# Moving the modulation columns of a two-layer decoder trunk between stages, and its first accumulating DMAs behind the sums of squares

## The chip, the core and the metric

The kernel runs on one core of a Trainium2 chip. The metric is device time in microseconds (us) of one execution. Five engines matter: PE (TensorE, the matmuls; PEld is its weight load), DVE (VectorE), ACT (ScalarE), POOL (GpSimd) and SP (SyncE, which here only issues DMAs). Each has its own list of instructions, fixed when the kernel is built, and goes through it in that order; a wait at the head of a list holds up what stands behind it.

## The reference

A decoder trunk of two layers on 1024 tokens of width 1024, in f32. Each layer is

```
mod = silu(c) @ ada_w[i] + ada_b[i];   sh1, sc1, g1, sh2, sc2, g2 = split(mod, 6)
h   = rmsnorm(x, norm1_g) * (1 + sc1) + sh1
x   = x + g1 * (mixers(h @ w_in) @ w_out)        # SSD scan, pooling, dilated attention
h   = rmsnorm(x, norm2_g) * (1 + sc2) + sh2
x   = x + g2 * (silu(g) * u @ ffn_down),  g, u = conv3(h @ ffn_up)
```

and a last rmsnorm. `mod` is a vector of 6144 numbers for each layer: 48 columns of 128 in the kernel, 8 columns for each of the six parts (part 0 is sh1, 1 sc1, 2 g1, 3 sh2, 4 sc2, 5 g2).

## The kernel before, in words

Activations lie transposed, 128 channels by 1024 tokens in a tile. A matmul in f32 is made of three with weights and activations split in a high and a low half: `hi*hi`, `hi*lo`, `lo*hi` (lines 232 to 234, or 966 to 968 in the up projection). Each weight block of 128x512 is loaded by SP, its high half is cast by ACT (L161) and its low half is subtracted by DVE (L162), so that ACT and DVE are busy beside PE all the time.

A layer has four stages. The **mixer** follows a table by hand, `ORDER`: projections of the input (tiles `qk`, `B`, `C`, `xs`, `z`, `u`), attention, scan, norm and pooling, interleaved. The **output projection** ends it: a first half (tile `dq`) in `accum_group`, a second half (`dn`) in `accum_last`. The latter goes over the eight blocks of x twice, once for each half of the tokens; each block's square is summed up for the rmsnorm (`square_add`, L187; on POOL for blocks 1 to 6, on DVE for block 7), and when the sum is done `rstd_begin` lets PE add it over partitions (tile `ssps`, L203). The **up projection** (`ffn`) runs 22 units f, in a form with seven half-size products each (tiles `px`, `pv`); a unit's convolutions, silu and product are four DVE instructions on `fg` and `fu` (L1120) and one product `fg*fu` (L1161) at its end, whose result goes to DRAM. The **down projection** reads it back, in five groups of `accum_group` (`dq`) and an `accum_last` (`dn`).

Four weights of a unit are sums of blocks of `ffn_up`, and are added by DMAs that accumulate, issued from POOL (`plus`, L1011): S1 and S3 each get a block added, S2 gets S1, S4 gets S2. `prepare(0)` and `prepare(1)` issue those of the first two units, eight in all, ahead of `accum_last` of the output projection.

A column of `mod` (`ada_col`, L137) takes two loads of 128x512 by SP (tile `araw`) and two DVE instructions (L143) that multiply and sum them up. `araw` takes one of the two buffers of `raw`, which it shares with the weight blocks; in the down projection it takes one of the 16 buffers of a ring (`wr`). Part 0 and 1 of layer 0 are made at the start by other means. The other 80 columns stand in these places:

- mixer of layer 0: 24 columns, parts 2, 4 and 3 of layer 0 (the `A` entries of `ORDER`)
- up projection of layer 0: 12 columns, one in each unit from 7 to 18: part 5 of layer 0, then the first four of layer 1
- down projection of layer 0: the other 44 of layer 1, in `accum_group` of the groups 1 to 4
- layer 1: none

The program is written in the order of the code, but the build's scheduler then sets each engine's list by priorities and modelled times, so that instructions stand earlier in the list than the code says where it finds the engine idle.

Of the kernel before, what the change touches and what calls it, by code (L numbers as in the profile page):

```python
# [8 lines left out]
F32 = mybir.dt.float32  # L9
# [45 lines left out]
def tile_trunk(ctx, tc, xT_d, c_d, ck_d, adas_d, pos_d, par_d, pff_d, fg_d, adaw_d, win_d, wv_d, poolw_d, wout_d, up_d, down2_d, down_d,  # L55
# [82 lines left out]
    def ada_col(l, j, take=None):  # L138

        for i in range(2):  # L140
            r = take("araw") if take else rawp.tile([128, 528], F32, tag="raw", name="araw")[:, 0:512]
            nc.sync.dma_start(r, adaw_d[l, j, :, HALF[i]])
            dve.scalar_tensor_tensor(r, r, 1.0, cact[:, HALF[i]], ALU.mult, ALU.mult,  # L143
                                     accum_out=mod[l][:, j:j + 1] if i == 0 else mod2[:, j % 8:j % 8 + 1])
        if j % 8 == 7:
            s = slice(j - 7, j + 1)
            dve.tensor_tensor(mod[l][:, s], mod[l][:, s], mod2, op=ALU.add)
            ada_fin(l, j // 8, 0, 8)
# [270 lines left out]
    def layer(l, hi, lo, end, st):  # L419
# [390 lines left out]
        todo = [p * 8 + k for p in (2, 4, 3) for k in range(8)] if l == 0 else []  # L810
# [29 lines left out]
        for t in ORDER.split():  # L840
            if t[0] in "BCXzu":
                project(t)
            elif t[0] == "A":
                for _ in range(int(t[1:])):
                    if todo:
                        ada_col(0, todo.pop(0))
# [22 lines left out]
    def ffn(l, ys, end):  # L869
# [134 lines left out]

        def prepare(f):
# [4 lines left out]
            def plus(t, src):  # L1010
                nc.gpsimd.dma_start(t, src, accum_op=ALU.add)  # L1011
# [119 lines left out]
        accum_last(wout_d[l, 1], ys, 16, l, None, PARTS[0], first_half, begin, second_half, store)  # L1131

        todo = [(0, 40 + k) for k in range(8)] + [(1, p * 8 + k) for p in (1, 0, 2, 4, 3, 5) for k in range(8)] if l == 0 else []

        def ada(n, take=None):
            for _ in range(n):
                if todo:
                    ada_col(*todo.pop(0), take)
# [25 lines left out]
        for f in range(NFF + 1):  # L1164
# [5 lines left out]
            if 6 < f < 19:  # L1170
                ada(1)
# [8 lines left out]
        for g, n in enumerate(GROUPS):  # L1180
# [4 lines left out]
            else:  # L1185
                m = acts(fs, ht) if g else m0
                for i, _ in enumerate(accum_group(down_d[l, g] if n == 4 else down2_d[l], m, 40, l, () if g else pre)):
                    if g:
                        ada(1 + (n > 2 and i % 2), wr)
# [26 lines left out]
    def accum_last(src, m, gcol, l, dep, parts, then, early, rest=None, store=None):  # L1216
# [4 lines left out]
        for hs in parts:  # L1221
            acc = p2("acc", "nr", 2)[:, 0:hs.stop - hs.start]
            for n in range(8):
# [9 lines left out]
                square_add(acc, x[n][:, hs], n == 0, nc.gpsimd if rest and n < 7 else dve)  # L1233
                if done and not early:
                    then(n, *done)
# [142 lines left out]
```

## Time and profile before

| | us |
|---|---|
| median of 3 runs | 2293.74 (2292.01 to 2296.97) |
| profiled execution | 2290.45 |
| its span, first to last instruction | 2288.6 |
| PE busy | 2227.4 (97%) |
| DVE busy | 1549.4 (68%) |
| ACT busy | 1058.9 (46%) |
| POOL busy | 242.4 (11%) |
| mean granted PE clock | 0.990 |

How to read it: "x24" is a count, "128x512" a tile's partitions and elements, "<-" leads from what is written to what is read. In a timeline row the first number is the start, the second the duration, and a bracket at its end gives the idle time of the engine just before it and what ended it. The two layers run the same stages one after the other, so that a stage of layer 0 can be set beside the same stage of layer 1.

### The profile page before, as it was taken

The numbers are of one execution on the slowest core, as the hardware profiler recorded it, in microseconds if no ns is written. First come the engines' busy times: TensorE is split into PE (matmuls) and PEld (weight loads), VectorE is DVE, ScalarE is ACT, GpSimd is POOL, SyncE is SP. The second block draws the span as 40 slices with busy tenths as digits, with TensorE's granted clock in tenths as the row PEclk, the third lists the DMA queues.
The fourth block names the chain that finished last, engine by engine and source line by source line (L and its number), as shares of the span: only waits on it lengthen the run. The fifth ranks groups of instructions, "written<-read, shape, count | busy, mean of one in ns | idle before, by whom it ended". The sixth has DMA issues, their size and how long they took to land.

```text
span 2288.6 us, 29727 instructions
## 1 busy us (share of the span) xinstructions
PE 2227.4 (97%) x10472; PEld 1809.1 (79%) x10472; DVE 1549.4 (68%) x2712; ACT 1058.9 (46%) x1960; POOL 242.4 (11%) x308
## 2 busy tenths in 40 slices
PE   6999999899999999999999999998999999999998
PEld 4878877687788888788888888776888888878887
DVE  6467887588766667995564577774976666675446
ACT  5366664355444545312244667533654554452212
POOL 0210000231111110000001000003211111100000
PEclk9999999999999999999999999998999999999999
DMA  7452333558787776992233211235777767673112
GB/s 274 126 150 77 95 111 127 161 147 223 209 201 176 176 174 193 340 310 63 58 132 109 57 55 48 83 107 173 178 186 179 179 171 180 162 246 103 50 46 88
DMA packets 186228, 338.93 MB, mean 148 GB/s; under 512 B 28704, under 2 KB 44320, under 8 KB 186080
## 3 DMA queue, kind: packets, MB, share of 16 engines
q1 hardware_dynamic: 126144, 244.44, 32.8%
q0 software_dynamic: 30560, 61.56, 14.9%
q10 hardware_dynamic: 29376, 31.05, 4.1%
q8 instruction: 82, 1.34, 0.2%
q14 instruction: 66, 0.54, 0.1%
HBM read 265.93 MB, written 44.83 MB: 136 GB/s over the span
## 4 chain that ended last, share of the span: by engine, by line
PE 67%; DVE 2%; DMA 2%; ACT 0%; issue 0%; POOL 0%; SPq 0%; ACTq 0%; DVEq 0%; POOLq 0%
PE dq L232 6%; PE dq L233 6%; PE dq L234 6%; PE px L966 6%; PE px L967 6%; PE px L968 6%; PE pv L966 4%; PE pv L967 4%; PE pv L968 4%; PE dn L234 1%; PE dn L232 1%; PE dn L233 1%; PE qk L232 1%; PE qk L233 1%; PE qk L234 1%; PE z L232 1%
## 5 line engine op out<-in xcount | busy, mean ns | idle before, releaser
L161 ACT CAST whi<-wraw 128x512 fp32r<-128x512 f32 (+2 forms) x196 | 117.6, 602 | 398.4 <-PE dq L233 268.3
L232 PE MATMUL dq<-ah,whi 128*128 128x512 f32 x576 | 226.9, 394 | 1.9 <-DVE xd L1213 1.2
L233 PE MATMUL dq<-al,whi 128*128 128x512 f32 x576 | 226.6, 393 | 0.0
L234 PE MATMUL dq<-ah,wlo 128*128 128x512 f32 x576 | 225.8, 393 | 0.0
L161 ACT CAST whi<-S 128x512 fp32r<-128x512 f32 x176 | 108.7, 620 | 213.8 <-PE px L967 124.5
L162 DVE TENSOR_TENSOR wlo<-wraw,whi 128x512 fp32r<-128x512 f32 (+2 forms) x196 | 132.0, 677 | 106.8 <-ACT whi L161 102.1
L1213 DVE SCALAR_TENSOR_TENSOR xd<-dq,mod,xd 128x1024 f32<-128x1024 f32 x80 | 102.7, 1284 | 127.1 <-PE dq L234 127.1
L162 DVE TENSOR_TENSOR wlo<-S,whi 128x512 fp32r<-128x512 f32 x176 | 120.8, 688 | 80.3 <-ACT whi L161 78.1
L966 PE MATMUL px<-T24h,whi 128*128 128x512 f32 x352 | 139.7, 397 | 4.7 <-ACT s L1029 3.2
L143 DVE SCALAR_TENSOR_TENSOR araw<-araw,cact 128x512 f32<-128x512 f32 x160 | 106.5, 690 | 52.9 <-DMA araw<-in_adaw 52.9
L968 PE MATMUL px<-T24h,wlo 128*128 128x512 f32 x352 | 138.9, 395 | 1.3 <-DVE wlo L162 1.3
L967 PE MATMUL px<-T24l,whi 128*128 128x512 f32 x352 | 139.0, 395 | 0.0
L966 PE MATMUL pv<-B,whi 128*128 128x512 f32 x344 | 135.7, 395 | 0.0
L967 PE MATMUL pv<-B,whi 128*128 128x512 f32 x344 | 135.5, 394 | 0.0
L968 PE MATMUL pv<-B,wlo 128*128 128x512 f32 x344 | 135.0, 393 | 0.0
L1120 DVE SCALAR_TENSOR_TENSOR fg<-G,pff,fg 128x1023 f32<-128x1023 f32 x88 | 112.7, 1281 | 26.5 <-ACT fg L1118 26.4
L232 PEld LDWEIGHTS dq<-ah,whi 128*128 128x128 f32 x576 | 108.3, 188 | 28.0 <-ACT whi L161 1.8
L161 ACT CAST whi<-A 128x512 fp32r<-128x512 f32 x118 | 73.2, 620 | 120.5 <-PE pv L967 58.0
L234 PEld LDWEIGHTS dq<-ah,wlo 128*128 128x128 f32 x576 | 108.3, 188 | 25.1 <-DVE wlo L162 0.5
L233 PEld LDWEIGHTS dq<-al,whi 128*128 128x128 f32 x576 | 108.4, 188 | 24.0
L162 DVE TENSOR_TENSOR wlo<-A,whi 128x512 fp32r<-128x512 f32 x118 | 81.0, 686 | 63.2 <-ACT whi L161 54.6
L1011 POOL DMA_DIRECT2D S<-S x88 | 75.4, 869 | 426.0 <-DMA S<-in_up 309.6
(403 smaller groups left out, 5883.1 us busy)
## 6 DMA issues: line engine op xcount, KB each, us to landing
S<-in_up SPq DMA_DIRECT2D x176, 256.0 KB, 3.1
araw<-in_adaw SPq DMA_DIRECT2D x160, 256.0 KB, 4.2
A<-in_up SPq DMA_DIRECT2D x118, 256.0 KB, 3.7
S<-in_up POOLq DMA_DIRECT2D x88, 256.0 KB, 5.5
S<-S POOLq DMA_DIRECT2D x88, 256.0 KB, 4.1
raw<-act_d SPq DMA_DIRECT2D x88, 256.0 KB, 4.1
act_d<-fg SPq DMA_DIRECT2D x40, 512.0 KB, 3.8
wraw<-in_down SPq DMA_DIRECT2D x80, 256.0 KB, 2.8
```

What stands on the lines that cost most here:

```text
L143: dve.scalar_tensor_tensor(r, r, 1.0, cact[:, HALF[i]], ALU.mult, ALU.mult, accum_out=mod[l][:, j:j + 1] if i == 0 else mod2[:, j % 8:j % ...
L161: act.copy(hi[:, 0:n], raw)
L162: dve.tensor_tensor(lo[:, 0:n], raw, hi[:, 0:n].bitcast(F32), op=ALU.subtract)
L232: mm(ps, wh, hi[k][:, s], start=i == 0, stop=False)
L233: mm(ps, wh, lo[k][:, s], start=False, stop=False)
L234: mm(ps, wl, hi[k][:, s], start=False, stop=i == n - 1)
L966: after(mm(ps, wh[:, c], h_, start=first and k == 0, stop=False, skip_group_check=not first), dep)
L967: mm(ps, wh[:, c], l_, start=False, stop=False, skip_group_check=not first)
L968: mm(ps, wl[:, c], h_, start=False, stop=k == 3, skip_group_check=not first)
L1011: nc.gpsimd.dma_start(t, src, accum_op=ALU.add)
L1120: dve.scalar_tensor_tensor(acc[:, s:T], t[:, 0:T - s], pff[:, (2 - s) * 44 + cc:(2 - s) * 44 + cc + 1], acc[:, s:T], ALU.mult, ALU.add)
L1213: group_last[0] = dve.scalar_tensor_tensor(x[n], ps, mod[l][:, gcol + n:gcol + n + 1], x[n], ALU.mult, ALU.add)
```

## The change

Two edits. The accumulating DMAs of units 0 and 1 are put on a list, `pending`, and taken off it one by one in `accum_last`, in its second half of the tokens, each behind a block's sum of squares. And the 80 columns are spread anew: mixer of layer 0 24 as before, up projection of layer 0 24 (units 3 to 20, two in every third), down projection none, mixer of layer 1 24, up projection of layer 1 8. All of them take the two `raw` buffers.

```
-        todo = [p * 8 + k for p in (2, 4, 3) for k in range(8)] if l == 0 else []
+        todo = [p * 8 + k for p in (2, 4, 3) for k in range(8)]
...
-                        ada_col(0, todo.pop(0))
+                        ada_col(l, todo.pop(0))
...
+        pending = []
+
+        def sums(part, n):
+
+            if part and pending and n < 7:
+                pending.pop(0)()
+                if n == 6:
+                    while pending:
+                        pending.pop(0)()
...
-                nc.gpsimd.dma_start(t, src, accum_op=ALU.add)
+                add = lambda: nc.gpsimd.dma_start(t, src, accum_op=ALU.add)
+                if f < 2:
+                    pending.append(add)
+                else:
+                    add()
...
-        todo = [(0, 40 + k) for k in range(8)] + [(1, p * 8 + k) for p in (1, 0, 2, 4, 3, 5) for k in range(8)] if l == 0 else []
+        todo = [(l, 40 + k) for k in range(8)] + ([(1, p * 8 + k) for p in (1, 0) for k in range(8)] if l == 0 else [])
...
-            if 6 < f < 19:
-                ada(1)
+            if 2 < f < 21:
+                ada(1 + (f % 3 == 0))
...
-                for i, _ in enumerate(accum_group(down_d[l, g] if n == 4 else down2_d[l], m, 40, l, () if g else pre)):
-                    if g:
-                        ada(1 + (n > 2 and i % 2), wr)
+                for _ in accum_group(down_d[l, g] if n == 4 else down2_d[l], m, 40, l, () if g else pre):
+                    pass
...
                 square_add(acc, x[n][:, hs], n == 0, nc.gpsimd if rest and n < 7 else dve)
+                if sums:
+                    sums(hs.start, n)
```

What the build makes of it in the engines' lists is seen at three places. First, POOL in the output projection of layer 1, before; `S..<-in_up` and `S..<-S..` are the accumulating DMAs of units 0 and 1, `acc` the sums of squares of the first half of the tokens:

```order
L1011 DMA S_13411<-in_up 128x512
L1011 DMA S_13415<-in_up 128x512
L1011 DMA S_13413<-S_13411 128x512
L187 TENSOR_TENSOR acc<-acc,sq 128x512
L1011 DMA S_13425<-in_up 128x512
L1011 DMA S_13422<-S_13413 128x512
L1011 DMA S_13429<-in_up 128x512
L1011 DMA S_13427<-S_13425 128x512
L187 TENSOR_TENSOR acc<-acc,sq 128x512 x2
L1011 DMA S_13436<-S_13427 128x512
L187 TENSOR_TENSOR acc<-acc,sq 128x512 x9
```

And the same place in the changed kernel:

```order
L1021 DMA S_13361<-in_up 128x512
L1021 DMA S_13365<-in_up 128x512
L1021 DMA S_13363<-S_13361 128x512
L187 TENSOR_TENSOR acc<-acc,sq 128x512
L1021 DMA S_13371<-in_up 128x512
L1021 DMA S_13369<-S_13363 128x512
L187 TENSOR_TENSOR acc<-acc,sq 128x512
L1021 DMA S_13375<-in_up 128x512
L1021 DMA S_13373<-S_13371 128x512
L187 TENSOR_TENSOR acc<-acc,sq 128x512
L1021 DMA S_13379<-S_13373 128x512
L187 TENSOR_TENSOR acc<-acc,sq 128x512 x9
```

Nine sums behind the last DMA are three of the first half of the tokens and the six of the second half. All eight DMAs stand ahead of those three, before and after; one sum stands two DMAs earlier. In layer 0 seven of the eight stand ahead of the first half's last two sums before, and of its last one after; the eighth stands behind all six in both.

Second, DVE in the up projection of layer 0, in the unit whose `fg*fu` is the eighth, before; `wlo` is the low half of a weight block:

```order
L162 TENSOR_TENSOR wlo_5693<-S3_5598,whi_5692 128x512
L162 TENSOR_TENSOR wlo_5712<-A12_5605,whi_5711 128x512
L162 TENSOR_TENSOR wlo_5729<-S1_5594,whi_5728 128x512
L1034 TENSOR_TENSOR G_5582<-pv_5565,U2_5500 128x512
L162 TENSOR_TENSOR wlo_5774<-A11_5754,whi_5773 128x512
```

And in the changed kernel:

```order
L162 TENSOR_TENSOR wlo_5729<-S3_5634,whi_5728 128x512
L143 SCALAR_TENSOR_TENSOR araw_6447,mod2_103<-araw_6447,cact_97 128x512
L143 SCALAR_TENSOR_TENSOR araw_6606,mod1_102<-araw_6606,cact_97 128x512
L162 TENSOR_TENSOR wlo_5748<-A12_5641,whi_5747 128x512
L143 SCALAR_TENSOR_TENSOR araw_6609,mod2_103<-araw_6609,cact_97 128x512
L162 TENSOR_TENSOR wlo_5765<-S1_5630,whi_5764 128x512
L143 SCALAR_TENSOR_TENSOR araw_6767,mod1_102<-araw_6767,cact_97 128x512
L1048 TENSOR_TENSOR G_5618<-pv_5601,U2_5536 128x512
L162 TENSOR_TENSOR wlo_5812<-A11_5792,whi_5811 128x512
L143 SCALAR_TENSOR_TENSOR araw_6770,mod2_103<-araw_6770,cact_97 128x512
```

Five column instructions now stand in this unit. Counted between one `fg*fu` and the next, the column instructions in layer 0 were 2, 2, 6, 5, 6, 3 and are now 2, 2, 6, 6, 5, 6, 5, 6, 5, 5; in layer 1 they were none and are now 2, 2, 6, 6.

Third, DVE in the mixer of layer 1, where `dts` is what ACT and PE wait for to begin the scan; before:

```order
L162 TENSOR_TENSOR wlo_10764<-wraw_10761,whi_10763 128x512
L518 COPY acs_10571<-acsps_10568 128x64
L162 TENSOR_TENSOR wlo_10770<-wraw_10767,whi_10769 128x512
L522 TENSOR_TENSOR dts_10575<-acsps_10568,acs_10571 128x64
L551 TENSOR_TENSOR kk0_10597<-qk1_10286,kk0_10597 64x1024
```

And in the changed kernel:

```order
L162 TENSOR_TENSOR wlo_10575<-wraw_10572,whi_10574 128x512
L518 COPY acs_10370<-acsps_10367 128x64
L162 TENSOR_TENSOR wlo_10581<-wraw_10578,whi_10580 128x512
L143 SCALAR_TENSOR_TENSOR araw_10735,mod1_102<-araw_10735,cact_97 128x512
L143 SCALAR_TENSOR_TENSOR araw_10738,mod2_103<-araw_10738,cact_97 128x512
L143 SCALAR_TENSOR_TENSOR araw_10791,mod1_102<-araw_10791,cact_97 128x512
L522 TENSOR_TENSOR dts_10374<-acsps_10367,acs_10370 128x64
L551 TENSOR_TENSOR kk0_10396<-qk1_10085,kk0_10396 64x1024
```

Three column instructions now stand ahead of `dts`, as they do in layer 0 (before and after). From the copy of `acs` to the start of the second half of the output projection, DVE's and PE's lists in the two layers of the changed kernel are the same, row for row, but for one small set-up instruction (L423, a 128x40 scaling for the next layer).

More of the change, by code (lines that the diff above doesn't have):

```diff
@@ L136, in tile_trunk, with ada_col @@
     act.activation(cact, cact, AF.Silu)
-    def ada_col(l, j, take=None):
+    def ada_col(l, j):
         for i in range(2):
-            r = take("araw") if take else rawp.tile([128, 528], F32, tag="raw", name="araw")[:, 0:512]
+            r = rawp.tile([128, 528], F32, tag="raw", name="araw")[:, 0:512]
             nc.sync.dma_start(r, adaw_d[l, j, :, HALF[i]])
@@ L1130, in ffn, with ada @@
         prepare(1)
-        accum_last(wout_d[l, 1], ys, 16, l, None, PARTS[0], first_half, begin, second_half, store)
-        todo = [(0, 40 + k) for k in range(8)] + [(1, p * 8 + k) for p in (1, 0, 2, 4, 3, 5) for k in range(8)] if l == 0 else []
-        def ada(n, take=None):
+        accum_last(wout_d[l, 1], ys, 16, l, None, PARTS[0], first_half, begin, second_half, store, sums)
+        todo = [(l, 40 + k) for k in range(8)] + ([(1, p * 8 + k) for p in (1, 0) for k in range(8)] if l == 0 else [])
+        def ada(n):
             for _ in range(n):
                 if todo:
-                    ada_col(*todo.pop(0), take)
+                    ada_col(*todo.pop(0))
         def acts(fs, pool):
@@ L1214, in accum_group, with accum_last @@
             yield
-    def accum_last(src, m, gcol, l, dep, parts, then, early, rest=None, store=None):
+    def accum_last(src, m, gcol, l, dep, parts, then, early, rest=None, store=None, sums=None):
         mh, ml = zip(*m)
```

## Prediction

> **What bounds the kernel now.** I read the page first: shares of the engines, the chain that ended last, the costliest groups.
>
> ```profile
> span 2288.6 us, 29727 instructions
> PE 2227.4 (97%) x10472; PEld 1809.1 (79%) x10472; DVE 1549.4 (68%) x2712; ACT 1058.9 (46%) x1960; POOL 242.4 (11%) x308
> PE 67%; DVE 2%; DMA 2%; ACT 0%; issue 0%; POOL 0%; SPq 0%; ACTq 0%; DVEq 0%; POOLq 0%
> L143 DVE SCALAR_TENSOR_TENSOR araw<-araw,cact 128x512 f32<-128x512 f32 x160 | 106.5, 690 | 52.9 <-DMA araw<-in_adaw 52.9
> ```
>
> PE sets the time, and is idle for 2288.6 - 2227.4 = 61.2 us. The change touches no matmul, so it can only open or close gaps on PE. A column is two of the L143 instructions, 0.69 us each, and the last figure is what counts: DVE stood still 52.9 us in front of them, waiting for their loads, with everything behind them in its list waiting too.
>
> The two layers run the same stages, layer 0 with columns, layer 1 with none. So I looked up where each stage begins, by the first matmul of its tile: scan part of the mixer (B), output projection (dn), up projection (px), down projection (dq), its last part (dn).
>
> ```profile
> L232 PE MATMUL B<-h1h,whi x32: 392/396/774, 112.1 to 223.6; 128*128 128x512 f32 x32
> L232 PE MATMUL dn<-yh,whi x32: 389/394/628, 424.0 to 468.5; 128*128 128x512 f32 x32
> L966 PE MATMUL px<-B,whi x80: 389/394/404, 480.3 to 895.7; 128*128 128x512 f32 x80
> L232 PE MATMUL dq<-ah,whi x288: 389/392/501, 918.6 to 1118.8; 128*128 128x512 f32 x144
> L232 PE MATMUL dn<-ah,whi x32: 389/394/481, 1119.5 to 1154.1; 128*128 128x512 f32 x32
> L232 PE MATMUL B<-h1h,whi x32: 387/396/482, 1236.9 to 1342.1; 128*128 128x512 f32 x32
> L232 PE MATMUL dn<-yh,whi x32: 389/393/628, 1538.9 to 1587.5; 128*128 128x512 f32 x32
> L966 PE MATMUL px<-B,whi x80: 389/394/404, 1599.3 to 2006.1; 128*128 128x512 f32 x80
> L232 PE MATMUL dq<-ah,whi x288: 389/392/469, 2029.0 to 2229.0; 128*128 128x512 f32 x144
> L232 PE MATMUL dn<-ah,whi x48: 276/283/404, 2229.7 to 2271.6; 128*128 128x256 f32 x32, 128*128 128x512 f32 x16
> ```
>
> Then the busy time of the engines in these stretches, layer 0 above layer 1 in each pair.
>
> ```profile
> core 0: us, PE busy (x) PEld busy (x) DVE busy (x) ACT busy (x) POOL busy (x), PEclk, DMA share, GB/s
> 112.10:424.00 311.90, 304.45 (x1602) 247.07 (x1602) 244.86 (x589) 183.56 (x442) 14.41 (x27) 0.98 0.36 108
> 1236.90:1538.90 302.00, 300.94 (x1603) 243.40 (x1603) 217.60 (x492) 186.66 (x444) 14.43 (x27) 1.00 0.25 73
> 424.00:480.30 56.30, 49.78 (x209) 40.02 (x208) 30.21 (x46) 19.36 (x33) 21.27 (x19) 0.94 0.64 180
> 1538.90:1599.30 60.40, 51.60 (x210) 41.56 (x209) 30.23 (x46) 19.30 (x33) 21.17 (x19) 0.89 0.57 168
> 480.30:918.60 438.30, 432.32 (x1866) 349.48 (x1865) 313.80 (x437) 226.41 (x341) 75.09 (x86) 1.00 0.75 193
> 1599.30:2029.00 429.70, 429.44 (x1865) 348.74 (x1864) 298.52 (x379) 228.01 (x342) 75.65 (x86) 1.00 0.71 183
> 918.60:1119.50 200.90, 199.97 (x865) 162.12 (x864) 152.84 (x305) 45.28 (x78) 1.05 (x2) 1.00 0.61 205
> 2029.00:2229.70 200.70, 199.69 (x866) 162.38 (x865) 100.20 (x121) 45.29 (x77) 0.55 (x1) 1.00 0.29 90
> ```
>
> This is an experiment already made. Same matmuls in each pair, and the columns' price is the difference: mixer 311.9 - 302.0 = 9.9 us for 24 columns; up projection 438.3 - 429.7 = 8.6 us for 12; down projection 200.9 - 200.7 = 0.2 us for nearly all of 44. In the down projection DVE was full of columns (152.8 against 100.2 us) and PE did not notice, since it needs DVE there only once in a block. The change takes the columns from the one stage where they are free.
>
> **The change part by part: columns in the up projection.** DVE's product fg*fu ends a unit, so its starts show how fast DVE goes from unit to unit. The first row is a stall of PE, the next are from DVE's timeline, the last from the instruction's statistics over a stretch without columns.
>
> ```profile
> 539.47 0.50 PE L966 MATMUL px<-T24h,whi 128*128 128x512 f32 x1 [1.50 <-ACT U L1029]
> 557.91 1.22 DVE L1161 TENSOR_TENSOR fg<-fg,fu 128x1024 f32<-128x1024 f32 x1
> 581.14 1.22 DVE L1161 TENSOR_TENSOR fg<-fg,fu 128x1024 f32<-128x1024 f32 x1
> 603.49 1.23 DVE L1161 TENSOR_TENSOR fg<-fg,fu 128x1024 f32<-128x1024 f32 x1
> 611.95 0.69 DVE L143 SCALAR_TENSOR_TENSOR araw<-araw,cact 128x512 f32<-128x512 f32 x1 [4.66 <-DMA araw<-in_adaw]
> 625.68 1.22 DVE L1161 TENSOR_TENSOR fg<-fg,fu 128x1024 f32<-128x1024 f32 x1
> 645.89 1.22 DVE L1161 TENSOR_TENSOR fg<-fg,fu 128x1024 f32<-128x1024 f32 x1
> 662.18 1.22 DVE L1161 TENSOR_TENSOR fg<-fg,fu 128x1024 f32<-128x1024 f32 x1
> L1161 DVE TENSOR_TENSOR fg<-fg,fu x13: 1220/1222/1233, 662.2 to 895.3; 128x1024 f32<-128x1024 f32 x13
> ```
>
> A clean unit takes (895.3 - 662.2) / 12 = 19.43 us, PE's pace. Units with 6, 5 and 6 column instructions took 23.23, 22.35 and 22.19 us, one with 3 took 20.21: DVE falls behind by 3.8, 2.9, 2.8 and 0.8, together 10.3, and catches up 3.1 in the next clean one (16.29). The reason is in the row at 611.95: two buffers hold two loads, the third column instruction of a unit waits for a load that could only be issued once the first was used. Late sums on DVE hold up ACT's copies and the weights' low halves, and PE stalls. Check: 10.3 - 3.1 and the stall of 1.5 at 539.47, which layer 1 lacks, make 8.7, against 8.6 measured.
>
> In the changed kernel the list has the same pattern, but for eight such units in layer 0 (6, 6, 5, 6, 5, 6, 5, 5) instead of 6, 5, 6, 3. Slack is spent by then, so each further unit costs what the last full one did, 22.19 - 19.43 = 2.8: four units 11.1, and the one with 3 becomes a full one, 2.0. Sum **+13.1 us**. Bounds: by the column, 12 x 8.6 / 12 = 8.6; by the slowest unit, 5 x 3.8 = 19.0.
>
> Layer 1 gets 2, 2, 6, 6: 3.8 + 2.9 - 3.1 caught up + 1.5 = **+5.1 us**. Bounds: 1.5, if the two full units fit into the slack, and 3.8 x 2 - 3.1 + 1.5 = 6.0.
>
> **Columns in the mixer.** Mixer 1 gets the 24 columns in mixer 0's very order, so I take mixer 0's time: **+9.9 us**. The first stall below says what that consists of (the other two rows are for the accumulating DMAs).
>
> ```profile
> 120.85 0.61 PE L529 MATMUL acsTp<-ident,acs 128*8 128x128 f32 x4 [3.23 <-DVE dts L522]
> 456.64 1.87 PE L203 MATMUL ssps<-ones,acc 128*128 128x1 f32 x8 [3.88 <-DVE acc L187]
> 1575.28 1.02 PE L203 MATMUL ssps<-ones,acc 128*128 128x1 f32 x4 [6.67 <-DVE acc L187]
> ```
>
> PE's idle time in mixer 0 is 311.90 - 304.45 = 7.45 us against 302.00 - 300.94 = 1.06 in mixer 1; the stall of 3.23 is `dts` queued behind three column instructions. The other 3.5 us lie in PE's busy time, with a granted clock of 0.98 against 1.00. The Trainium skill (TensorE: Matmul & The Clock Gate, What's actually happening) has the clock fall only after an idle window of about 3.4 us; by that these 3.5 us would not come again and the term would be 6.4. Here the clock fell although the longest stall of the stage lasted 3.23 us. Bounds: 6.4, the idle time alone; above, 12, if the weight loads that share the two buffers come later still.
>
> **Down projection.** 44 columns out: 0.2 us back, at most 200.90 - 199.97 = 0.9, PE's whole idle time there. DVE's 52.6 us that go away lay beside PE's matmuls; nobody there waits for them.
>
> **Accumulating DMAs.** What they cost is seen on POOL in the output projection of layer 1 (start, duration, idle before):
>
> ```profile
> 1561.54 0.99 POOL L1011 DMA_DIRECT2D S<-S  x1
> 1562.11 3.13 POOL L187 TENSOR_TENSOR acc<-acc,sq 128x512 f32<-128x512 f32 x2
> 1569.65 0.87 POOL L1011 DMA_DIRECT2D S<-S  x1 [4.42 <-DMA S<-S]
> 1570.26 4.24 POOL L187 TENSOR_TENSOR acc<-acc,sq 128x512 f32<-128x512 f32 x3
> ```
>
> The last issue must wait until the one of 1561.54 has landed, 8.1 us later; three sums stand behind it, then DVE's, then PE's 6.67 us of stall. The code now issues these DMAs behind the second half's sums, but the build's list still has all of them, that issue included, ahead of the same three sums. The DMA it waits for moves behind one more sum, so its landing slips by up to 1.4 us (4.24 / 3), about +0.9 in layer 1. In layer 0 one sum less stands behind the seventh DMA, about -0.9. Taken as **0**, from -2.8 to +2.8 (one sum in each layer, either way). POOL's own list has nothing else there, and units 0 and 1 use these weights only after 480.3.
>
> **Sum.** 13.1 + 5.1 + 9.9 - 0.2 + 0 = +27.9 us. The profiled execution took 2290.45 us (span 2288.6 and 1.85 around it), so 2318.35 on its scale; the median of the runs, 2293.74, lies 3.29 above it, and with that the forecast is **2321.6 us**, 1.2% slower.
>
> **The rivals.** First, the sums come free: if the eight DMAs do go late, PE's 3.88 and 6.67 go, 10.6, and with them part of what the clocks of 0.94 and 0.89 take off 56.3 and 60.4 us (3.4 and 6.6): about -14, that is 2307.6. For it, the stalls are real; against it, POOL's list, in which nothing decisive moved. Still slower. 5%.
>
> Second, only busy time counts: DVE was busy 313.8 of 438.3 us in the up projection and 244.9 of 311.9 in mixer 0, so columns fit everywhere and the +8.6 and +9.9 are layer 0's own (its first units, its tables). Then the result is 2293.5, no change. The Trainium skill (Perfetto Trace Analysis, Identifying the Most-Contended Engine) says that for VectorE the occupancy is a fair measure of how close it is to its limit; by that page this rival would hold. The trace speaks against it: a DVE busy at 72% was late by 2.8 us and more in each full unit, because it waits in order. 5%.
>
> Third, on the other side, loads that arrive in time: DVE's waits for `araw` vanish in the up projections because SP's list differs a little. The point is the third load of a unit: it would have to land before 607.3 (611.95 - 4.66), where DVE ran dry, not at 611.95. Then layer 0's 8.6 us go as well, layer 1 pays nothing, and mixer 1 pays its idle time without the stall behind the loads, 6.4 - 3.2 = 3.2: 2293.74 - 8.6 + 3.2 - 0.2 = 2288.1, faster by 0.25%. Against it: still two buffers, still six instructions in a unit. 5%.
>
> **How the numbers follow.** The forecast, columns paid as in layer 0, has 85%. Its low ends add to 8.6 + 1.5 + 6.4 - 0.9 - 2.8 = 12.8, its high ends to 19.0 + 6.0 + 12 + 2.8 = 39.8. The range is 2306 to 2334, which takes in the first rival. A measurement of this kernel can tell about 0.2%, 4.6 us, from no change: slower 0.90 (forecast and first rival), same 0.05 (second), faster 0.05 (third).
>
> **What would show it.** Right: DVE's fg*fu at 22 us distance over eight units of layer 0, with 4 to 5 us waits for `araw` in each; the up projection of layer 0 near 451 us and of layer 1 near 435, mixer 1 near 312 with PE stalled some 3 us at `acsTp`; down projections alike at 200.7; stalls at `ssps` still 3 to 4 and 6 to 7 us. Wrong: distances back at 19.4 us after the first units (columns then cost by start-up, not by number), mixer 1 still near 302, or `ssps` without its wait.

## The result and the profile after

The changed kernel takes 2317.73 us (median; 2315.3 to 2320.89) against 2294.67 us of the kernel before, run beside it: a ratio of 1.0104, 95% interval 1.0092 to 1.0115, that is 23 us slower. The forecast was 2321.6 us, and slower. The profiled execution of the changed kernel took 2315.77 us, 25.3 more than that of the kernel before.

The page of the changed kernel, three of its lines: the span, the busy times, and the group of the column instructions.

```profile
span 2314.0 us, 29734 instructions
PE 2236.5 (97%) x10472; PEld 1815.9 (78%) x10472; DVE 1549.0 (67%) x2712; ACT 1054.1 (46%) x1958; POOL 242.3 (10%) x308
L143 DVE SCALAR_TENSOR_TENSOR araw<-araw,cact 128x512 f32<-128x512 f32 x160 | 109.2, 688 | 105.8 <-DMA araw<-in_adaw 105.5
```

The number of instructions on PE and DVE and the busy time of DVE are what they were. What doubled is the idle time in front of the column instructions, from 52.9 to 105.8 us. PE's idle time went from 61.2 to 77.5 us (2314.0 - 2236.5), and PE's busy time rose by 9.1 us for the same matmuls.

The stages of the changed kernel, cut at the first matmul of each as in the prediction, mixer, output, up and down projection, layer 0 above layer 1 in each pair:

```profile
core 0: us, PE busy (x) PEld busy (x) DVE busy (x) ACT busy (x) POOL busy (x), PEclk, DMA share, GB/s
112.10:423.30 311.20, 303.14 (x1602) 245.88 (x1602) 244.85 (x589) 183.78 (x442) 14.41 (x27) 0.99 0.36 108
1248.60:1559.30 310.70, 303.48 (x1604) 246.08 (x1603) 244.47 (x588) 183.76 (x442) 14.42 (x27) 0.99 0.36 108
423.30:480.00 56.70, 51.30 (x209) 41.57 (x208) 30.27 (x46) 19.46 (x33) 21.19 (x19) 0.91 0.63 179
1559.30:1620.00 60.70, 51.80 (x210) 41.66 (x209) 30.25 (x46) 19.32 (x33) 21.13 (x19) 0.89 0.58 166
480.00:930.70 450.70, 437.66 (x1866) 352.33 (x1865) 326.82 (x482) 224.96 (x342) 75.59 (x86) 0.98 0.77 202
1620.00:2053.80 433.80, 430.19 (x1865) 348.76 (x1864) 307.98 (x413) 227.28 (x342) 75.67 (x86) 1.00 0.74 190
930.70:1131.30 200.60, 199.59 (x865) 162.41 (x864) 100.41 (x122) 45.17 (x77) 0.55 (x1) 1.00 0.28 91
2053.80:2254.50 200.70, 199.69 (x866) 162.47 (x865) 100.14 (x121) 45.35 (x77) 0.55 (x1) 1.00 0.29 91
```

The second figure of a row is the stage's length. Three stages grew: the up projection of layer 0 from 438.3 to 450.7 (+12.4), mixer 1 from 302.0 to 310.7 (+8.7), the up projection of layer 1 from 429.7 to 433.8 (+4.1). The down projection of layer 0, freed of 52 us of DVE's work, is at 200.6 where it was at 200.9. That is +24.9 of the +25.4 us of the span.

DVE's timeline in the up projection of layer 0, the products that end a unit and two of the waits between them (in brackets the wait before the instruction):

```profile
557.67 1.22 DVE L1175 TENSOR_TENSOR fg<-fg,fu 128x1024 f32<-128x1024 f32 x1
...
581.79 1.22 DVE L1175 TENSOR_TENSOR fg<-fg,fu 128x1024 f32<-128x1024 f32 x1
...
591.49 0.69 DVE L143 SCALAR_TENSOR_TENSOR araw<-araw,cact 128x512 f32<-128x512 f32 x1 [6.05 <-DMA araw<-in_adaw]
...
605.14 1.22 DVE L1175 TENSOR_TENSOR fg<-fg,fu 128x1024 f32<-128x1024 f32 x1
...
635.21 0.69 DVE L143 SCALAR_TENSOR_TENSOR araw<-araw,cact 128x512 f32<-128x512 f32 x1 [5.74 <-DMA araw<-in_adaw]
...
737.09 1.23 DVE L1175 TENSOR_TENSOR fg<-fg,fu 128x1024 f32<-128x1024 f32 x1
751.95 1.22 DVE L1175 TENSOR_TENSOR fg<-fg,fu 128x1024 f32<-128x1024 f32 x1
771.35 1.22 DVE L1175 TENSOR_TENSOR fg<-fg,fu 128x1024 f32<-128x1024 f32 x1
```

From 557.67 to 737.09 lie the eight units with five or six column instructions: 22.43 us each, against 19.4 behind them. One clean unit then catches up 4.6 us (14.86).

The unit that begins at 581.79 shows what is waited for. Its first two column instructions, and SP's asking for the next two loads (`x2`, the second at 585.28):

```profile
582.92 0.68 DVE L143 SCALAR_TENSOR_TENSOR araw<-araw,cact 128x512 f32<-128x512 f32 x1
584.14 0.68 DVE L143 SCALAR_TENSOR_TENSOR araw<-araw,cact 128x512 f32<-128x512 f32 x1
584.63 1.83 SPq L142 DMA_DIRECT2D araw<-in_adaw x2
```

The third column instruction starts at 591.49, 6.9 us after its load was asked for, and that load was asked for only after the first instruction had used its buffer.

PE's stalls at the places that the prediction named, in the changed kernel (start, duration, in brackets the idle time):

```profile
455.92 1.85 PE L203 MATMUL ssps<-ones,acc 128*128 128x1 f32 x8 [2.80 <-DVE acc L187]
1257.48 0.60 PE L529 MATMUL acsTp<-ident,acs 128*8 128x128 f32 x4 [3.28 <-DVE dts L522]
1595.87 1.87 PE L203 MATMUL ssps<-ones,acc 128*128 128x1 f32 x8 [6.78 <-DVE acc L187]
```

The wait for `dts` is now in mixer 1 too, and both waits for the sums of squares are still there, that of layer 0 a little under the 3 to 4 us named.

### The profile page after: what moved, and what is told of

Read it like the earlier page. It is cut to its first block, busy times and chain, and to the rows that moved or that the text cites. A ratio compares the mean times of both kernels' runs of the same rounds, so it can differ in the third digit from the quotient of the medians.

```text
span 2314.0 us, 29734 instructions
## 1 busy us (share of the span) xinstructions
PE 2236.5 (97%) x10472; PEld 1815.9 (78%) x10472; DVE 1549.0 (67%) x2712; ACT 1054.1 (46%) x1958; POOL 242.3 (10%) x308
## 5 line engine op out<-in xcount | busy, mean ns | idle before, releaser
L143 DVE SCALAR_TENSOR_TENSOR araw<-araw,cact 128x512 f32<-128x512 f32 x160 | 109.2, 688 | 105.8 <-DMA araw<-in_adaw 105.5
L1021 POOL DMA_DIRECT2D S<-in_up x88 | 80.9, 924 | 371.7 <-DMA S<-in_up 261.6
```

Source lines behind the costliest of these rows:

```text
L1021: add = lambda: nc.gpsimd.dma_start(t, src, accum_op=ALU.add)
```

## The experiments

The theory: a column costs nothing by its busy time. It costs where several stand in one stretch of DVE's list, because their loads go through two buffers and DVE waits for them in order, with the up projection's own work behind. The rivals were the busy time, the bandwidth of the loads, and the sums of squares coming free. In the diffs `after(a, b)` holds a behind b in their engine's list, and `done[0]` is a unit's product `fg*fu`. The stages in the table are from the profiled executions.

| run | us, median | before, beside it | ratio, 95% interval | out 0 | up 0 | mixer 1 | out 1 | up 1 |
|---|---|---|---|---|---|---|---|---|
| before | 2293.74 | | | 56.3 | 438.3 | 302.0 | 60.4 | 429.7 |
| after | 2317.73 | 2294.67 | 1.0104, 1.0092 to 1.0115 | 56.7 | 450.7 | 310.7 | 60.7 | 433.8 |
| columns_only | 2317.99 | 2293.09 | 1.0108, 1.0091 to 1.0125 | 56.7 | 449.8 | 310.7 | 60.8 | 438.4 |
| dmas_only | 2291.72 | 2293.09 | 0.9987, 0.9977 to 0.9997 | 52.8 | 440.2 | 303.3 | 60.7 | 430.0 |
| same_place_with_loads | 2313.36, one run | 2293.09 | | 56.4 | 447.3 | 313.3 | 61.3 | 433.3 |
| same_place_no_loads | 2284.39, one run | 2293.09 | | 58.5 | 429.1 | 307.3 | 61.1 | 430.1 |
| paced | 2291.14 | 2293.63 | 0.9984, 0.9974 to 0.9994 | 57.4 | 429.3 | 311.1 | 60.8 | 430.0 |
| short_columns | 2319.80 | 2294.80 | 1.0114, 1.0096 to 1.0132 | 53.7 | 449.8 | 315.4 | 62.7 | 434.3 |
| quarter_loads | 2294.37 | 2294.84 | 1.0001, 0.9990 to 1.0012 | 54.9 | 441.1 | 308.5 | 59.3 | 429.7 |
| mixer1_only | 2299.82 | 2293.63 | 1.0027, 1.0017 to 1.0037 | 56.6 | 435.4 | 311.2 | 59.1 | 429.5 |
| late_dmas | 2302.98 | 2293.63 | 1.0036, 1.0021 to 1.0051 | 47.4 | 458.9 | 310.6 | 46.3 | 439.9 |
| late_only | 2280.78 | 2294.80 | 0.9939, 0.9922 to 0.9957 | 47.1 | 446.5 | 304.0 | 46.5 | 432.8 |
| pace_only | 2283.99 | 2294.80 | 0.9957, 0.9942 to 0.9972 | 53.6 | 429.4 | 302.0 | 61.1 | 430.0 |
| paced_late | 2271.07 | 2293.63 | 0.9898, 0.9883 to 0.9914 | 47.1 | 434.9 | 302.7 | 46.1 | 433.1 |

A stage's length differs between profiled executions even where its column instructions are spread over the units alike: 438.3, 440.2 and 435.4 us for the up projection of layer 0 in before, dmas_only and mixer1_only, 433.8 and 438.4 for that of layer 1 in after and columns_only. So a difference under some 5 us in an up projection is not to be read from one row alone.

**Each half alone.** The first run has only the new places of the columns, the second only the edit of the accumulating DMAs:

```
columns_only, against after:
-                add = lambda: nc.gpsimd.dma_start(t, src, accum_op=ALU.add)
-                if f < 2:
-                    pending.append(add)
-                else:
-                    add()
+                nc.gpsimd.dma_start(t, src, accum_op=ALU.add)
dmas_only, against before: the same lines the other way, with sums() and its call
```

> The changed kernel with the accumulating DMAs back where they were: the columns' move alone. Theory (columns cost where DVE waits for their loads): all of the change, +23 us against the kernel before, up projections about 450 and 434 us, mixer 1 about 311. Rival (the DMAs' move gives or takes a few us): this kernel would lie over 3 us away from the changed one.

> The kernel before with only the accumulating DMAs put behind the second half's sums in the code. Theory (the build's list leaves them ahead of the sums): within 2 us of the kernel before, PE's stalls at ssps still 3 to 4 and 6 to 7 us. Rival (the sums come free): about 14 us faster, stalls at ssps under 1 us.

The columns alone bring the whole 25 us. The DMAs alone bring 0.1%, where the first rival of the prediction wanted 14 us. What was expected of the two stalls missed, though:

```profile
455.36 1.05 PE L203 MATMUL ssps<-ones,acc 128*128 128x1 f32 x8 [0.34 <-DVE acc L187]
1576.33 1.87 PE L203 MATMUL ssps<-ones,acc 128*128 128x1 f32 x8 [7.45 <-DVE acc L187]
```

In layer 0, where one sum less now stands behind the seventh DMA, the stall is nearly gone, and the output projection is 3.5 us shorter. With the same edit it is 2.80 us in the changed kernel, and without it 1.52 (pace_only) to 4.01 (mixer1_only), so how much of this is the edit's stays open. In the whole little of it is seen.

**The same instructions with and without their loads.** Both runs have the columns of the changed kernel in the up projections, put by force behind the product of a unit, six column instructions in each of eight units of layer 0. The second leaves out the loads and lets the same DVE instruction multiply what is already there:

```
same_place_with_loads, against columns_only:
-            dve.scalar_tensor_tensor(r, r, 1.0, cact[:, HALF[i]], ALU.mult, ALU.mult,
+            after(dve.scalar_tensor_tensor(r, r, 1.0, cact[:, HALF[i]], ALU.mult, ALU.mult,
...
-            if 2 < f < 21:
-                ada(1 + (f % 3 == 0))
+            if 2 < f < 11:
+                ada(3)
same_place_no_loads, against that:
-            nc.sync.dma_start(r, adaw_d[l, j, :, HALF[i]])
-            after(dve.scalar_tensor_tensor(r, r, 1.0, cact[:, HALF[i]], ALU.mult, ALU.mult,
+            after(dve.scalar_tensor_tensor(r, cact[:, HALF[1 - i]], 0.001, cact[:, HALF[i]], ALU.mult, ALU.mult,
```

> The control of the run below: columns as in the changed kernel, but each put behind a unit's fg*fu by an order on DVE alone: six column instructions in each of eight units of the up projection of layer 0, 6, 6 and 4 in layer 1. Theory (DVE waits for loads that two buffers hold back): the up projection of layer 0 near 450 us, DVE waiting over 40 us for araw in it. Rival (the changed kernel's places are what costs): near 430.

> As the control, at the same places, but the columns' loads are left out; the two DVE instructions of a column multiply halves of silu(c) that are there, so these columns of the modulation are not the reference's. Theory (the wait for the loads costs, not DVE's busy time): up projection of layer 0 near 430 us (427 to 433), of layer 1 near 430. Rival (DVE's 0.7 us instructions are too many): as the control, near 450. Mixer 1: by the theory its part that waits goes, 302 to 308 us; by the rival 311.

The up projection of layer 0 without the loads, by engine (columns as in the table of stages):

```profile
477.00:906.00 429.00, 429.00 (x1865) 348.63 (x1864) 327.37 (x481) 228.09 (x341) 75.21 (x86) 1.00 0.71 182
```

PE has no idle time in 429.00 us, and DVE was busy for 327.37 us, as long as with the loads (327.72). So the busy time of the columns costs nothing in the up projection, and what goes with their loads costs 18 us there. In the mixer it is otherwise: mixer 1 takes 313.3 us with the loads and 307.3 without. The stall at `acsTp` goes with the loads (3.20 us with them, under 0.5 without), but 5.3 us over the 302.0 of a mixer without columns stay. There about half of the cost is not the loads', and the theory holds for the up projections alone.

**The loads kept, and spread.** The changed kernel's number of columns in each stage, with the original accumulating DMAs, but two column instructions to a unit (four in every third), each behind its unit's product:

```
-                    ada_col(*todo.pop(0))
+                    ada_col(*todo.pop(0), done[0])
```

> The changed kernel's columns, in the same layers, but in the up projections they are spread evenly: two column instructions in a unit (four in every third), held behind that unit's product of gate and value, from unit 3 to unit 20, where the changed kernel has them in clusters. The accumulating DMAs stand as before the change. My theory: a unit can take as many columns without a wait as there are buffers for their loads (two instructions' worth), because these loads have the time of a whole unit, 19.4 us, to land; the third and later ones of a unit wait for a load issued only when a buffer came free. So the up projection of layer 0 falls from 450.7 to 430 to 438 us, that of layer 1 stays near 430 to 434, mixer 1 stays at 310 to 313, and the whole is 2300 to 2307 us. Rival, the loss is the columns' busy time or the bandwidth of their loads, which pacing does not change: up projection of layer 0 at 448 to 452 us and the whole at 2315 to 2319 us.

What SP's loads and DVE's waits look like in that stage, first in the changed kernel (the column loads, their time to landing, who waited for them), then in the spread one:

```profile
L142 SPq DMA_DIRECT2D araw<-in_adaw x48: 327/328/1719, 486.9 to 724.9; - x48
...
  DVE araw L143: 52.8, 19
...
DMA to landing us min/median/max: 2.4/4.5/7.4
```

```profile
L142 SPq DMA_DIRECT2D araw<-in_adaw x48: 327/328/1287, 488.8 to 853.0; - x48
...
  DVE araw L143: 7.8, 7
...
DMA to landing us min/median/max: 2.9/4.4/6.4
```

The same 48 loads take as long to land, 4.4 against 4.5 us, but DVE waits 7.8 us for them in place of 52.8, since most are asked for a unit ahead. PE is busy for the whole of the stage's 429.30 us:

```profile
482.00:911.30 429.30, 429.30 (x1866) 348.60 (x1865) 327.68 (x482) 227.77 (x342) 75.58 (x86) 1.00 0.80 212
```

The DMAs moved more in a microsecond here (212 GB/s) than in the changed kernel (202), so it was not the bandwidth of the stage as a whole. The total of 2291 us came out below the 2300 to 2307 expected. This stage fell to 429.3 and that of layer 1 to 430.0, at or just under the low ends of their ranges, which by themselves allowed 2293 (2317.7 - 20.7 - 3.8): the range of the total did not follow from those of the stages.

No run changes the number of buffers. The nearest is the down projection of layer 0 before the change, where the same instructions go through 16 of them: from 900 to 1120 us 88 of them waited 8.5 us in all for their loads, against 52.8 us for 48 in the changed kernel's up projection. The work around them differs, so this supports the two buffers' part and does not measure it.

**What the waits are made of.** In the first of two runs the column instruction reads 8 of its 512 elements and the loads stay whole. In the second both have 128 elements:

```
short_columns, against after:
-            dve.scalar_tensor_tensor(r, r, 1.0, cact[:, HALF[i]], ALU.mult, ALU.mult,
+            dve.scalar_tensor_tensor(r[:, 0:8], r[:, 0:8], 1.0, cact[:, 0:8], ALU.mult, ALU.mult,
quarter_loads, against after:
-            nc.sync.dma_start(r, adaw_d[l, j, :, HALF[i]])
-            dve.scalar_tensor_tensor(r, r, 1.0, cact[:, HALF[i]], ALU.mult, ALU.mult,
+            nc.sync.dma_start(r[:, 0:128], adaw_d[l, j, :, HALF[i]][:, 0:128])
+            dve.scalar_tensor_tensor(r[:, 0:128], r[:, 0:128], 1.0, cact[:, 0:128], ALU.mult, ALU.mult,
```

> The changed kernel with all its loads, but each column instruction reads only 8 of its 512 elements, so that the modulation is left incomplete and VectorE is rid of nearly all the busy time of the columns. My theory: most of what the columns cost is the wait for a load that could be issued only when a buffer came free, so that it stays in large part, less the time in which a buffer is held (the instruction itself, 0.7 us): up projection of layer 0 at 438 to 447 us, mixer 1 at 306 to 309, the whole at 2298 to 2308 us. Rival, the busy time: up projection of layer 0 at 428 to 431 us, mixer 1 at 302 to 304, the whole at 2278 to 2290 us. Second rival, the bandwidth of the loads: everything stays, 2314 to 2319 us.

> The changed kernel with each column instruction's load and the instruction itself cut to the first 128 of the 512 elements (64 KB in place of 256 KB), so that the modulation is left incomplete; number and places of loads and instructions and the two buffers stay. The control is the run in which the instructions alone were cut to 8 elements and the loads were whole: 449.8 us in the up projection of layer 0, 315.4 in mixer 1, 2319.8 in all. What stays after that run is why a cluster's loads are waited for. Theory, the bytes: six or so loads of 256 KB that are asked for within one unit, beside the weights' loads, land one pair after another, each pair 7 to 9 us after it was asked for; with a quarter of the bytes they land sooner, the up projection of layer 0 falls to 429 to 437 us, mixer 1 to 302 to 307, the whole to 2280 to 2298 us. Rival, the turn: a load is asked for only when the instruction before has freed a buffer and stands behind other loads in SyncE's row, whatever its size; then the up projection stays at 442 to 450 us, mixer 1 at 310 to 315, the whole at 2308 to 2320 us.

The group of the column instructions with 8 elements, in the whole program:

```profile
L143 DVE SCALAR_TENSOR_TENSOR araw<-araw,cact 128x8 f32<-128x8 f32 x160 | 24.8, 164 | 155.4 <-DMA araw<-in_adaw 155.0
```

Busy time fell by 84.4 us (109.2 to 24.8), the wait rose by 49.6 (105.8 to 155.4), and the kernel was no faster. Here the theory's own numbers failed: it had 438 to 447 us for the up projection of layer 0 and 306 to 309 for mixer 1, and 449.8 and 315.4 were measured. The shorter instruction did not bring the next load sooner: the loads of the up projection took 4.6 us to land (median) against 4.5, and DVE waited 64.5 us for them there. That outcome is the second rival's in this run, yet the spread loads have ruled out bandwidth as an average. The second run asks how much of it is bytes. Its column loads in the up projection of layer 0:

```profile
  DVE araw L143: 46.9, 24
...
DMA to landing us min/median/max: 1.8/3.3/6.7
```

With a quarter of the bytes the up projection of layer 0 is at 441.1 us and mixer 1 at 308.5, between the two ranges that were expected for each; the whole, 2294.37, lies in the theory's. How much of this is the bytes can't be read from the stage's length, since the instructions did not stay in their places: the build put seven column instructions into each of six units, where the changed kernel has five or six in each of eight. The products at both ends of these six units:

```profile
553.28 1.23 DVE L1175 TENSOR_TENSOR fg<-fg,fu 128x1024 f32<-128x1024 f32 x1
...
684.53 1.22 DVE L1175 TENSOR_TENSOR fg<-fg,fu 128x1024 f32<-128x1024 f32 x1
```

A unit takes 21.88 us, 2.4 above a clean one, where the changed kernel's takes 3.0 above it. By that (an estimate, since the units hold seven instructions here) about a fifth of a unit's cost went with three quarters of the bytes, and the rest of what the stage gained goes with there being two such units fewer. Most of the cost stays with loads of a quarter of the size: in each of the six units one of them was still waited for 3.3 to 6.6 us. In mixer 1 6.5 us over 302.0 stay, of the changed kernel's 8.7.

**Mixer 1 alone.** The kernel before, with only the 24 columns of the mixer of layer 1 moved there:

```
-        todo = [p * 8 + k for p in (2, 4, 3) for k in range(8)] if l == 0 else []
+        todo = [p * 8 + k for p in (2, 4, 3) for k in range(8)]
...
-        todo = [(0, 40 + k) for k in range(8)] + [(1, p * 8 + k) for p in (1, 0, 2, 4, 3, 5) for k in range(8)] if l == 0 else []
+        todo = [(0, 40 + k) for k in range(8)] + [(1, p * 8 + k) for p in (1, 0, 5) for k in range(8)] if l == 0 else []
```

> The kernel before, with one of the two moves alone: the 24 columns of layer 1 that the mixer needs (parts 2, 4 and 3) are computed in mixer 1; the others stay in the up and down projections of layer 0. The accumulating DMAs stand as before. My theory: mixer 1 grows from 302.0 to about 311 us and nothing else moves, so that the whole is 8.7 to 9.9 us slower than before: 2302 to 2303 us. Rival, the columns in the mixer are hidden and what the changed kernel lost there came from what was moved around them: 2293 us, no change. Second rival, the down projection of layer 0 gets shorter by the busy time that it is rid of (24 columns): then mixer 1's loss is partly repaid and the whole stands at 2296 to 2299 us.

The stage is at 311.2 us, +9.2 as expected. The whole is only 6.2 us slower (1.0017 to 1.0037), since the up projection of layer 0 came out 2.9 us shorter and the output projection of layer 1 1.3 shorter in the profiled execution. The down projection gave nothing back (200.6), so the second rival's reason doesn't hold, though its number lies nearer. What shortened those two stages is open: they hold the same number of columns as before, and both differences lie within what such stages vary by.

**Accumulating DMAs that truly come later.** In POOL's list of the changed kernel the DMAs still stood ahead of the first half's last sums. Here they are held behind the last of these, once in the changed kernel (late_dmas) and once in the kernel before (late_only):

```
-                add = lambda: nc.gpsimd.dma_start(t, src, accum_op=ALU.add)
+                add = lambda: after(nc.gpsimd.dma_start(t, src, accum_op=ALU.add), sum_last[0])
```

> The changed kernel with one thing more: the accumulating DMAs of the first two units are made to follow the last sum of squares of the first half on POOL, so that they truly come later in POOL's row (six sums, then the DMAs, then the second half's sums), where in the changed kernel the first half's sums still stand behind them. My theory: what PE loses on these sums in the changed kernel is 2.8 us in the output projection of layer 0 and 6.8 us in that of layer 1; with the sums ahead, both stalls go, but the second half's sums now stand behind a chain of landings, so that a part comes back: 2308 to 2316 us against 2317.7. Rival 1, the sums come free and nothing is given back: 2304 us (14 us less). Rival 2, the whole of it is given back in the second half: 2316 to 2320 us, with the stall at ssps in its place or moved by one group.

> The kernel before with the other thing alone: the accumulating DMAs of the first two units truly follow the first half's sums of squares on POOL. My theory: the two effects add, so that this one has what is left of the 22.6 us: 2278 to 2283 us, the two output projections shorter by about 9 and 14 us, the up projection of layer 0 longer by 5 to 8 us and that of layer 1 by 3 to 6. Rival, the effects overlap (both remove the same idle time of PE): 2272 to 2276 us.

POOL in the output projection of layer 1, first in the changed kernel (start, duration, in brackets the wait before):

```profile
1590.24 0.87 POOL L1021 DMA_DIRECT2D S<-S  x1 [4.85 <-issue]
1590.85 4.24 POOL L187 TENSOR_TENSOR acc<-acc,sq 128x512 f32<-128x512 f32 x3
```

and with the DMAs held back, in the kernel before:

```profile
1561.17 1.29 POOL L187 TENSOR_TENSOR acc<-acc,sq 128x512 f32<-128x512 f32 x1 [1.31 <-ACT sq L186]
1562.41 3.57 POOL L1026 DMA_DIRECT2D S<-in_up  x4
...
1578.66 0.85 POOL L1026 DMA_DIRECT2D S<-S  x1 [2.04 <-DVE B L904]
1579.23 9.91 POOL L187 TENSOR_TENSOR acc<-acc,sq 128x512 f32<-128x512 f32 x6
```

Now the first half's sums are through before the first DMA, and the second half's six stand behind the last, which goes out 16.3 us after the first. The output projections fall by 9.2 and 13.9 us, and the up projections, which the second half's sums lead into, give back 8.2 and 3.1; in layer 0 the stall at `ssps` is found again there:

```profile
477.23 1.84 PE L205 MATMUL ssps<-ones,acc 128*128 128x1 f32 x8 [3.24 <-DVE acc L187]
```

A part of what the output projections gain is slower matmuls that are gone: in late_only PE is busy for 46.69 of 47.10 and 46.50 of 46.50 us at a granted clock of 1.00 in both, where the kernel before had 49.78 of 56.30 and 51.60 of 60.40 us at 0.94 and 0.89.

The net is 14.0 us against the kernel before, and 14.8 against the changed kernel by medians of different sets of runs (2302.98 and 2317.73). By the profiled executions, whose own time varies by a few us, it is 11.0 and 7.9. late_dmas came out below the 2308 to 2316 expected, at rival 1's size of 14 us; but rival 1 had nothing given back, and its stages show a part given back. The size fits it better than my number, the mechanism less.

**The version that beats both.** The kernel before with the columns of its up projection spread one to a unit, alone and together with the late DMAs:

```
pace_only, against before:
-                    ada_col(*todo.pop(0), take)
+                    ada_col(*todo.pop(0), take, None if take else done[0])
paced_late, against that:
-                nc.gpsimd.dma_start(t, src, accum_op=ALU.add)
+                add = lambda: after(nc.gpsimd.dma_start(t, src, accum_op=ALU.add), sum_last[0])
...
```

> The kernel before with one thing alone: the twelve columns (two instructions each) that it computes in the up projection of layer 0 are held behind the product of gate and value of their own unit, one column to a unit; the accumulating DMAs stand as before. My theory: the up projection of layer 0 falls from 438.3 to 429 to 431 us, as even spacing gave it with twice the columns, and no other stage moves: 2284 to 2287 us against 2293.7. Rival, the gain of the version with both edits came from the sums alone: 2292 to 2295 us.

> A version meant to beat both: the columns stand where the kernel before has them (up projection and down projection of layer 0, none in mixer 1), but the twelve column instructions that a few units of the up projection held in clusters are spread two to a unit behind that unit's product; and the accumulating DMAs truly follow the first half's sums on POOL. My theory: the up projection of layer 0 falls from 438.3 to about 430 us, and the output projections lose the PE stalls at the sums of squares (2.8 and 6.8 us) in part: 2276 to 2286 us, against 2293.7 of the kernel before. Rival, pacing brings nothing there and the sums' stalls are given back in the second half: 2290 to 2295 us.

Spreading alone takes the up projection of layer 0 to 429.4 us and the whole 10.8 us down. Against what was expected other stages moved too in the profiled execution: the output projection of layer 0 was 2.7 us shorter, the down projection 1.9 longer (202.8). The two together are 22.6 us faster than the kernel before (1.0%), a little less than their sum of 24.8. The expected 2276 to 2286 was too careful: the output projections gave 9.2 and 14.3 us, more than the stalls of 2.8 and 6.8 us that were counted (in the kernel before they are 3.88 and 6.67).

## Why the prediction was right, point by point

**Columns in the up projection of layer 0**: +13.1 forecast, +12.4 measured. The eight units were there, with the waits that were named (the longest of a unit 3.5 to 6.1 us, where 4 to 5 was said), and cost 22.43 - 19.43 = 3.0 us each where the forecast had 2.8 for each further one. What DVE fell behind (8 x 3.0, less 4.6 caught up) and the stall of 1.5 us make 20.9, against 450.7 - 429.7 = 21.0 over layer 1 before the change. The mechanism, a third load that is asked for late and waited for in order, is shown by the runs without loads and with spread loads, and by the rows at 582.92 to 591.49. It was incomplete in one thing: what a wait is made of. The third load is asked for 1.7 us after the first instruction starts, and the wait of 6.05 us lies wholly within the 6.9 us until it has landed. With a quarter of the bytes a unit still costs 2.4 us. That two buffers are too few is argued from the order of these rows; no run has more of them in this stage.

**Columns in the up projection of layer 1**: +5.1 forecast, +4.1 measured. The size is less certain than that looks: with the same columns, the run of the columns alone had +8.7 in its profiled execution, above the bound of 6.0.

**Columns in mixer 1**: +9.9 forecast, +8.7 measured (8.6 to 9.2 in four other runs with the same columns and loads there: columns_only, paced, mixer1_only, late_dmas; 11.3 in same_place_with_loads). The stall of 3.28 us at `acsTp` came as said. PE's idle time is 310.70 - 303.48 = 7.2 us, near the 7.45 of layer 0 before, and the busy time rose by 2.5 with the clock at 0.99. By the Trainium skill (TensorE: Matmul & The Clock Gate, What's actually happening) the term would have been 6.4; the trace disagrees with that again: no stall of the stage is longer than 3.28 us. The forecast took the term over from mixer 0 as a whole; the waits that it named are only a part of it, since 5.3 us stay in the run without loads.

**Down projection**: -0.2 forecast, -0.3 measured.

**Accumulating DMAs**: 0 forecast; dmas_only gives -1.4 us by medians, and -3.0 with an interval of -5.3 to -0.7 by the ratio, so that it may lie a little outside the bounds of 2.8. POOL's list, not the diff, told that the edit hardly moved what mattered. With the move made in earnest the whole gained the first rival's 14 us, but that is luck: the output projections gained 23.1 us where it had 14, and 11.3 came back in the up projections.

**Sum**: +27.9 forecast, +25.3 in the profiled executions, +23.1 by medians. All three terms of columns were taken a little too high, by 0.7, 1.0 and 1.2 us. The rest of the 4.8 us by medians is where the two profiled executions stand to their medians, 4.2 us below for before and 2.0 below for after.

**The second rival**, that only busy time counts, fell, though in the mixer a part of the cost stays without the loads. The Trainium skill (Perfetto Trace Analysis, Identifying the Most-Contended Engine) takes VectorE's occupancy as a fair measure of its nearness to its limit; in the changed kernel DVE was busy for 326.82 of 450.7 us and its waits cost PE 21 us, while the spread run, with DVE busy for 327.68 of 429.30 us, cost nothing. Here the occupancy does not tell the two apart.

## What to carry to other kernels

Before moving side work to another stage, look at what waits there in order: work that is free in a stage that needs an engine once in a block can cost about three microseconds a unit in one that needs it all the time, at the same busy time. Spread such work at the pace at which its buffers refill, and hold it to its place in the built list, since the order in the code is not the order on the engine. Read that list for whether an edit has moved what it was meant to move: here the late DMAs were worth 0.1% as built, and 14 us when held in place.

## What the runs showed of the hardware

A good part of what DVE's lateness costs PE is not idle time. PE's busy time in the up projection of layer 0 is 437.66 us in the changed kernel and 429.30 in the spread one, for 1866 matmuls each: 8.4 of the 21.4 us between the two are slower matmuls. Slices of 10 us of the changed kernel show where (the third column is PE's busy time and matmuls, the third from the end the granted clock):

```profile
core 0: us, PE busy (x) PEld busy (x) DVE busy (x) ACT busy (x) POOL busy (x), PEclk, DMA share, GB/s
600.00:610.00 10.00, 7.57 (x25) 5.74 (x26) 8.94 (x16) 3.81 (x7) 1.70 (x2) 0.83 0.66 178
610.00:620.00 10.00, 10.00 (x45) 8.17 (x44) 5.78 (x11) 4.21 (x6) 1.71 (x2) 1.00 0.88 231
...
640.00:650.00 10.00, 6.81 (x25) 4.63 (x23) 8.08 (x11) 5.12 (x9) 0.85 (x1) 0.86 0.78 201
650.00:660.00 10.00, 9.80 (x35) 7.88 (x36) 5.27 (x11) 2.88 (x6) 0.85 (x1) 0.80 0.75 210
```

In the slice from 600 us 25 matmuls took 7.57 us, 0.30 each, where 45 took 10.00, 0.22 each, in the next. The stalls there are short:

```profile
600.49 0.50 PE L968 MATMUL px<-T24h,wlo 128*128 128x512 f32 x1 [1.86 <-DVE wlo L162]
605.02 0.50 PE L966 MATMUL px<-T24h,whi 128*128 128x512 f32 x1 [1.94 <-ACT s L1043]
645.67 0.50 PE L968 MATMUL px<-T24h,wlo 128*128 128x512 f32 x1 [2.28 <-DVE wlo L162]
```

The longest is 2.28 us, and the granted clock still went to 0.80 to 0.86 in these slices. The Trainium skill (TensorE: Matmul & The Clock Gate, What's actually happening) has an idle window of about 3.4 us for that; the trace shows it after shorter ones. Finer slices show that one such stall is enough, and how deep the clock falls:

```profile
646.00:647.00 1.00, 1.00 (x6) 0.81 (x5) 1.00 (x3) 0.00 (x0) 0.00 (x0) 1.00 0.85 139
647.00:654.00 7.00, 5.89 (x15) 4.14 (x14) 6.97 (x11) 3.05 (x5) 0.30 (x1) 0.51 0.55 180
654.00:660.00 6.00, 6.00 (x27) 4.85 (x27) 1.30 (x3) 1.73 (x3) 0.56 (x1) 1.00 0.85 219
```

The stall of 2.28 us that ends at 645.67 is the first over 0.2 us since 605.02. Some 1.4 us behind it the granted clock is at half, for about 7 us, into which a further stall of 1.11 us falls. After the stall of 1.86 us that ends at 600.49 the clock stayed at 1.00 until 606; it fell only behind the second one, of 1.94 us. Whether that one would have done it alone is not settled.
